# Seven opening pairs of a joint MLP over six PSUM banks in place of two, with twelve small operations on GpSimd in place of VectorE and two more tiles for sums

## The chip, the core and the metric

The kernel runs on one core of a Trainium2 chip. The metric is device time in microseconds for one launch; lower is better. The engines are named as the profile names them: PE is TensorE's matmul (PEld its weight load), DVE is VectorE, ACT is ScalarE, POOL is GpSimd, SP is SyncE, which here only issues DMAs.

## What is computed

One layer of a bidirectional encoder on 2048 tokens of 1024 features, in float32: a mixer of attention and convolution, a cross attention, a squared-ReLU MLP, and a final RMSNorm. The change lies in the MLP:

```python
u = rmsnorm(h, norm_mlp_g[l]) @ w_up[l]            # (2048, 1024) @ (1024, 4096)
h = h + jnp.square(jax.nn.relu(u)) @ w_down[l]     # (2048, 4096) @ (4096, 1024)
return rmsnorm(h, norm_final_g)
```

## The kernel before

The 2048 tokens are handled as four passes of 512 tokens. Everything is kept transposed: a tile has 128 features on its partitions and 512 tokens along its free axis. Passes 0 and 1 have an MLP each. Passes 2 and 3 share one, the joint MLP, which multiplies a 2 x 2 block matrix of weights by a 2 x 2 block matrix of activations with seven block products in place of eight (the Strassen-Winograd scheme).

**Operands.** Each product is done in three matmuls of half-width numbers: every operand is split into a high part (float16) and a low part (the rest, float16), and high x high, high x low and low x high are summed in PSUM. `prod` (lines 1788 to 1792) does one block product: four k steps of 128 features by three matmuls, 12 matmuls of 128 x 512, all into one PSUM bank.

**The seven blocks of activations** are b11, b21 (pass 2, its first and last 512 features), b22 (pass 3, its last 512 features) and four sums t1, t2, t3, t4. Each has four k tiles, and each k tile a high tile `Y..h` and a low tile `Y..l`. b11 and b21 are made while pass 2 is finished. The other five are made in the loop over k at lines 1768 to 1786, once pass 3's norm is known. For each k this loop makes two normalized tiles `n[0]`, `n[1]` (line 1772), then t1 = n0 - yn2 (1775), t2 = n1 - t1 (1776), t3 = n1 - n0 (1781), t4 = yn2' - t2 (1784), all on VectorE, and splits b22, t2, t1, t3 and t4 with `split_to` (lines 1723 to 1725): ScalarE copies the tile to float16 (1724), VectorE subtracts this from the tile and writes the low part (1725). The tiles for n and the sums come from `yt_` (line 1760), six buffers under one tag; each k needs six.

**Opening pairs.** The 4096 columns of `w_up` are handled as 16 pairs: a column block i of 128 with block i + 16. The loop at lines 1894 to 1898 runs ahead of the main loop for the first PRO = 7 pairs, with the part that needs only b11 and b21, so that it can run before the five other blocks exist. For each pair:

- the weight tile is loaded and split into high and low parts (`wpair`, lines 1798 on ScalarE and 1799 on VectorE); the even pairs have two buffers in one pool and the odd pairs two in another;
- `first_product` (1822): `prod` of b11 into a bank of kind `b1`, then ScalarE copies the bank to the tile `c1` (1826), which a GpSimd DMA writes to memory;
- `second_product` (1829): `prod` of b21 on top, in the same bank; then `squared` (1811): ScalarE takes the Relu from the bank (1812), which is the bank's last reader, and squares it (1813) into the tile `r11`, which a GpSimd DMA writes to memory.

The tiles c1 and r11 share six buffers (`wt_`). The kind `b1` has the banks 0 and 1, used in turn.

**Main loop.** `up_pair` (1836) runs for all 16 pairs. It loads two weight tiles, forms sums of them on VectorE (1844 to 1848), splits three sets (uu for t4; us for t2 and t1; ut for t3 and b22) and runs the products t4, then of the pair before the last product (`rest`, b22), then t2, t1, t3, with banks 2 and 3 (`b2`), 4 and 5 (`b3`), 6 and 7 (`b4`). For the first seven pairs it reads c1 and r11 back; for the others it runs the first and second product itself.

**Order.** The program text doesn't set the order of work. The kernel is traced, and a planner orders each engine's instructions by their place in the text and by a timeline that it simulates; each engine then runs its own list in that order and waits on semaphores where an operand or a buffer isn't there yet. An instruction that waits holds up all that stand behind it on its engine. A change in the buffers or in the engine of an operation can so give another order from there on.

**Memory.** The pool of the blocks and the pool `pm` of the working tiles stand where the pools of the closed stage `dense` stood.

Of the kernel before, what the change touches and what calls it, by code (L numbers as in the profile page):

```python
# [10 lines left out]
F32 = mybir.dt.float32  # L11
# [5 lines left out]
ALU = mybir.AluOpType  # L17
# [4 lines left out]
P = 128  # L22
# [25 lines left out]
def hybrid_layer(ctx, tc, A, out):  # L48
    nc = tc.nc
    ACT, DVE, POOL, PE = nc.scalar, nc.vector, nc.gpsimd, nc.tensor  # L50

    def pool(name, space=None, stack=ctx, side="left"):
        kw = {"reuse_waits": "tile", "side": side} if space is None else {"space": space}
        return stack.enter_context(tc.tile_pool(name=name, bufs=1, **kw))

    def dma(o, i, q=None):
        return (q or nc.sync).dma_start(o, i)  # L57
# [7 lines left out]
    banks = {"mm": (0, 1, 2, 5), "a": (3, 4), "sq": (6,), "c": (7,)}  # L65
# [199 lines left out]
    def wcols(w, c0, n=P, rows=None):  # L265
        v = w.rearrange("(k p) m -> p k m", p=P)
        return v[:, :, c0:c0 + n] if rows is None else v[:, rows[0]:rows[1], c0:c0 + n]
# [1446 lines left out]
    Y = {}  # L1714

    def half_room(pl, shape, **kw):
        t = pl.tile([shape[0], 2 * shape[1]] + list(shape[2:]), F16, **kw)
        return t[:, 0:shape[1]]
# [4 lines left out]
    def split_to(b, k, src):  # L1723
        ACT.copy(Y[b]["h"][k], src)
        DVE.tensor_tensor(Y[b]["l"][k], src, Y[b]["h"][k], op=ALU.subtract)
# [29 lines left out]
    pm = pool("up_work", stack=y_st)  # L1755

    def wt_(name, dtype=F32):
        return pm.tile([P, 512], dtype, tag="w", name=name, bufs=6)

    def yt_(name):  # L1760
        return pm.tile([P, 512], F32, tag="y", name=name, bufs=6)

    def late_tile(b, k):
        t = Y.setdefault(b, {"h": [], "l": []})
        for q in "hl":
            t[q].append(half_room(ybl[0], [P, 512], tag=f"{b}{q}{k}", name=f"Y{b}{q}{k}"))

    for k in range(4):
        n = [yt_(f"yn3_{k}{i}") for i in range(2)]
        for i in range(2):  # L1770
            kk = 4 * i + k
            DVE.scalar_tensor_tensor(n[i], h3[kk], gml[:, kk:kk + 1], rsbs[3], op0=ALU.mult, op1=ALU.mult)
        split_to("b22", k, n[1])
        t1b, t2b = yt_(f"yt1_{k}"), yt_(f"yt2_{k}")
        DVE.tensor_tensor(t1b, n[0], yn2[k], op=ALU.subtract)
        DVE.tensor_tensor(t2b, n[1], t1b, op=ALU.subtract)
        split_to("t2", k, t2b)
        late_tile("t1", k)
        split_to("t1", k, t1b)
        t3b = yt_(f"yt3_{k}")  # L1780
        DVE.tensor_tensor(t3b, n[1], n[0], op=ALU.subtract)
        split_to("t3", k, t3b)
        t4b = yt_(f"yt4_{k}")
        DVE.tensor_tensor(t4b, yn2[4 + k], t2b, op=ALU.subtract)
        late_tile("t4", k)
        split_to("t4", k, t4b)

    def prod(o, w, b, first):
        for k in range(4):
            for x, (i, q) in enumerate(((0, "h"), (0, "l"), (1, "h"))):  # L1790
                PE.matmul(o, w[i][:, k, :], Y[b][q][k], start=first and k + x == 0, stop=k == 3 and x == 2,
                          skip_group_check=not first)

    def halves(t):
        return [tuple(x[:, 4 * i:4 * i + 4, :] for x in t) for i in range(2)]
# [5 lines left out]
    def wpair(pl, t, name, shape=(P, 8, P)):  # L1801
        hi, lo = (half_room(pl, shape, tag=f"w{q}", name=f"w{q}_{name}", bufs=2) for q in ("hi", "lo"))
        scaled(hi, lo, t, mc[:, 0:1])
        return hi, lo

    def wraw(src, name):
        raw = wp.tile([P, 8, P], F32, tag="raw", name=f"raw_{name}", bufs=2)
        dma(raw, src)
        return raw

    def squared(r, src, j):
        ACT.activation(r, src, AF.Relu, scale=mc[:, 6:7])
        ACT.activation(r, r, AF.Square, accum_out=racc[:, j:j + 1])

    def keep_r(b, i, t):
        dma(rscr[b, i], t, nc.gpsimd)
# [5 lines left out]
    def first_product(i, a11):  # L1822
        b1 = ps("b1", f"b1_{i}")
        prod(b1, a11, "b11", True)
        c1 = wt_(f"c1_{i}")
        ACT.copy(c1, b1)
        return b1, c1

    def second_product(i, b1, a12):
        prod(b1, a12, "b21", False)  # L1830
        r11 = wt_(f"r11_{i}")
        squared(r11, b1, 4 * i)
        keep_r("b11", i, r11)
        return r11
# [56 lines left out]
        return rest  # L1891

    early_pairs = [True] * PRO
    for i in range(PRO):
        a1, a2 = halves(wpair(wq if i % 2 else wp, wraw(wcols(w_up, i * P), f"ua{i}"), f"ua{i}"))
        b1, c1 = first_product(i, a1)
        dma(cscr1[i], c1, nc.gpsimd)
        second_product(i, b1, a2)
    prev = lambda: None
    for i in range(NP):  # L1900
        prev = up_pair(i, early_pairs[i] if i < PRO else None, prev)
# [204 lines left out]
```

## Time and profile before

| | us |
|---|---|
| median of 3 runs | 2777.54 |
| lowest and highest of the runs | 2776.03, 2783.64 |
| the profiled execution, its time | 2774.07 |
| its span in the profile | 2772.3 |

The profiled execution is one execution on its own, and the views give positions in microseconds from the start of its span. A row of the order of time has the start, the duration, the engine, the line of the kernel, the operation, the tile written and the tiles read (buffer numbers left out), and in square brackets how long the engine had stood idle before it and what ended that. A row of groups has busy time and the mean duration of one behind the first bar, and idle time ahead of them behind the second. Matmuls overlap: one lasts 0.38 us, and the next starts 0.22 us after it. The opening pairs' first matmul starts at 2136.87; the main loop's last ends at about 2442.

### The profile page before, as it was taken

How to read it: one execution, taken by the hardware profiler on the slowest of the kernel's cores; microseconds unless marked ns; L12 is line 12 of the kernel's file. 1: busy time of each engine (PE TensorE's matmuls, PEld its weight loads, DVE VectorE, ACT ScalarE, POOL GpSimd, SP SyncE). 2: the span in 40 equal slices, each digit the busy share in tenths (PEclk: the TensorE clock that was granted, in tenths of full speed). 3: DMA queues.
4: the chain of work that ended last, by engine and by line, in shares of the span. 5: the costliest groups of instructions: out<-in, count | busy, mean ns of one | idle time of the engine just before them, and what ended most of it. 6: DMA issues, size and time to landing. Idle time of an engine off the chain costs nothing.

```text
span 2772.3 us, 40744 instructions
## 1 busy us (share of the span) xinstructions
PE 2661.1 (96%) x14787; PEld 1831.0 (66%) x14787; DVE 1918.8 (69%) x3508; ACT 1359.5 (49%) x2354; POOL 589.4 (21%) x807
## 2 busy tenths in 40 slices
PE   7899999988999999999999999999999999989998
PEld 4444457876777878788777777877887444434444
DVE  4568726665788876578976477756475887767776
ACT  6742217655454333434455555564343545545445
POOL 6474313543102212200111201121010122200000
PEclk9999999999999999999999999999999999999999
DMA  7874457887636666766457766764633564485553
GB/s 252 217 200 113 135 182 200 244 238 229 200 114 204 203 220 208 246 215 208 133 177 225 240 210 201 238 226 158 190 114 126 178 205 167 168 304 170 171 189 110
DMA packets 459816, 535.68 MB, mean 193 GB/s; under 512 B 98172, under 2 KB 329200, under 8 KB 459616
## 3 DMA queue, kind: packets, MB, share of 16 engines
q1 hardware_dynamic: 420992, 406.52, 48.5%
q0 software_dynamic: 36752, 123.06, 12.7%
q10 hardware_dynamic: 1872, 3.52, 0.3%
q8 instruction: 116, 1.90, 0.3%
q14 instruction: 84, 0.69, 0.1%
HBM read 384.46 MB, written 148.52 MB: 192 GB/s over the span
## 4 chain that ended last, share of the span: by engine, by line
PE 60%; DMA 13%; issue 11%; ACT 5%; DVE 5%; POOL 4%; SPq 2%; POOLq 0%; ACTq 0%; DVEq 0%
PE dn L270 4%; PE dn L271 4%; PE dn L272 4%; PE up L270 3%; PE up L272 3%; PE up L271 3%; PE lin L270 2%; PE lin L272 2%; PE lin L271 2%; SPq L57 2%; PE x L270 2%; PE x L271 2%; PE x L272 2%; PE xs L270 2%; PE xs L272 2%
## 5 line engine op out<-in xcount | busy, mean ns | idle before, releaser
L287 DVE SCALAR_TENSOR_TENSOR cacc<-cu,cwu,cacc 128x512 f32<-128x512 f32 x480 | 395.6, 826 | 6.8
L1032 ACT ACTIVATE sm<-sm,o 128x256 f32<-128x256 f32 (+1 forms) x384 | 159.2, 466 | 115.3 <-DVE o L1031 114.8
L270 PE MATMUL dn<-hhh,whi_d 128*128 128x512 f32 x512 | 202.1, 405 | 5.8 <-ACT hhh L1591 3.5
L270 PE MATMUL up<-mh,whi_u 128*128 128x512 f32 x512 | 203.9, 399 | 1.7 <-ACT whi_u L1567 1.7
L271 PE MATMUL dn<-hhl,whi_d 128*128 128x512 f32 x512 | 200.6, 394 | 0.8 <-DVE hhl L1592 0.8
L272 PE MATMUL up<-mh,wlo_u 128*128 128x512 f32 x512 | 200.0, 391 | 0.0
L272 PE MATMUL dn<-hhh,wlo_d 128*128 128x512 f32 x512 | 199.9, 393 | 0.0
L271 PE MATMUL up<-ml,whi_u 128*128 128x512 f32 x512 | 199.6, 390 | 0.0
L1042 DVE TENSOR_TENSOR pl<-pt,ph 128x512 f16<-128x512 f32 x160 | 109.6, 685 | 80.3 <-ACT ph L1041 79.8
L1031 DVE CUSTOM_DVE_ANT_0 sm<-s,mask 128x256 f32<-128x256 f32 (+1 forms) x384 | 126.6, 373 | 33.5 <-DMA oscr<-o 11.8
L1041 ACT CAST ph<-pt 128x512 f16<-128x512 f32 x160 | 92.2, 576 | 77.0 <-PE pt L1038 76.3
L1606 DVE TENSOR_TENSOR h<-h,dn 128x512 f32<-128x512 f32 x128 | 85.9, 682 | 55.6 <-PE dn L272 55.0
L247 POOL TENSOR_TENSOR nr<-st_v,mhalf 128x4 f32<-128x4 f32 x12 | 13.2, 1098 | 513.2 <-DVE st_v L243 513.2
L270 PEld LDWEIGHTS dn<-hhh,whi_d 128*128 128x128 f32 x512 | 95.5, 188 | 25.8 <-ACT hhh L1591 5.2
L272 PEld LDWEIGHTS dn<-hhh,wlo_d 128*128 128x128 f32 x512 | 96.6, 189 | 20.3
L270 PEld LDWEIGHTS up<-mh,whi_u 128*128 128x128 f32 x512 | 96.2, 188 | 20.6 <-ACT whi_u L1567 2.0
L271 PEld LDWEIGHTS dn<-hhl,whi_d 128*128 128x128 f32 x512 | 96.7, 189 | 19.6 <-DVE hhl L1592 1.8
L272 PEld LDWEIGHTS up<-mh,wlo_u 128*128 128x128 f32 x512 | 96.1, 188 | 20.5
L271 PEld LDWEIGHTS up<-ml,whi_u 128*128 128x128 f32 x512 | 96.3, 188 | 18.6
L270 PE MATMUL o<-cath,whi_o 128*128 128x512 f32 x256 | 103.0, 403 | 4.3 <-ACT whi_o L261 3.6
L272 PE MATMUL o<-cath,wlo_o 128*128 128x512 f32 x256 | 101.5, 398 | 1.4 <-DVE wlo_o L262 1.4
L1038 PE MATMUL pt<-ident,sm 128*128 128x128 f32 x640 | 100.1, 274 | 2.7 <-ACT sm L1032 2.5
(647 smaller groups left out, 7835.8 us busy)
## 6 DMA issues: line engine op xcount, KB each, us to landing
raw_u<-in_w_up_dram SPq DMA_DIRECT2D x64, 512.0 KB
raw_d<-in_w_down_dram SPq DMA_DIRECT2D x64, 512.0 KB
k<-kscr SPq DMA_DIRECT2D x32, 640.0 KB
raw_a<-ascr SPq DMA_DIRECT2D x32, 512.0 KB
raw_b<-bscr SPq DMA_DIRECT2D x32, 512.0 KB
lou<-wlo_u POOLq DMA_DIRECT2D x32, 512.0 KB, 5.4
lod<-wlo_d POOLq DMA_DIRECT2D x32, 512.0 KB, 5.5
wlo_u<-lou SPq DMA_DIRECT2D x32, 512.0 KB
```

Source lines behind the costliest of these rows:

```text
L57: return (q or nc.sync).dma_start(o, i)
L247: last["pow"] = POOL.tensor_tensor(dst, v, mhalf.to_broadcast([P, v.shape[1]]), op=ALU.pow)
L270: PE.matmul(o, lh, rh, start=first, stop=False)
L271: PE.matmul(o, lh, rl, start=False, stop=False)
L272: last["pe"] = PE.matmul(o, ll, rh, start=False, stop=end)
L287: DVE.scalar_tensor_tensor(acc, u[:, t:t + 512], cwu[:, c, t:t + 1], acc, op0=ALU.mult, op1=ALU.add)
L1031: last["dve"] = DVE.tensor_tensor_reduce(dst, so, mask[:, 256 * m:256 * m + nk], 1.0, 3e38, ALU.add, ALU.min, mn)
L1032: last["act"] = ACT.activation(dst, dst, AF.Exp, bias=mn, scale=-1.0)
L1038: last["pe"] = PE.transpose(pt[:, j, :], sm[:, j, :], ident)
L1041: ACT.copy(ph, pt)
L1042: DVE.tensor_tensor(pl, pt, ph, op=ALU.subtract)
L1606: last["dve"] = DVE.tensor_tensor(hs[m], hs[m], pt, op=ALU.add)
```

## The change

Four things change: VectorE's subtraction that makes a low part is done by GpSimd for the blocks b22 and t3, four tiles each (`split_by_pool`); the difference t3 = n1 - n0 is done by GpSimd, four times; the buffers of `yt_` become eight; and the opening pairs use six banks for `b1`, 0 to 5 in turn, after which `b1` has 0 and 1 again. The copies to float16 stay on ScalarE. Pair 6 is then the first to use a bank for the second time.

```diff
+    YB = 8
+
     def yt_(name):
-        return pm.tile([P, 512], F32, tag="y", name=name, bufs=6)
+        return pm.tile([P, 512], F32, tag="y", name=name, bufs=YB)
...
+    def split_by_pool(b, k, src):
+        ACT.copy(Y[b]["h"][k], src)
+        POOL.tensor_tensor(Y[b]["l"][k], src, Y[b]["h"][k], op=ALU.subtract)
+
     for k in range(4):
...
-        split_to("b22", k, n[1])
+        split_by_pool("b22", k, n[1])
...
-        DVE.tensor_tensor(t3b, n[1], n[0], op=ALU.subtract)
-        split_to("t3", k, t3b)
+        POOL.tensor_tensor(t3b, n[1], n[0], op=ALU.subtract)
+        split_by_pool("t3", k, t3b)
...
     early_pairs = [True] * PRO
+    banks.update(b1=(0, 1, 2, 3, 4, 5))
     for i in range(PRO):
...
         second_product(i, b1, a2)
+    banks.update(b1=(0, 1))
     prev = lambda: None
```

## The prediction

> **What bounds the kernel now.** I read the page first, then the stretch of the seven opening pairs and what follows, in windows (columns: from and to, length, then the busy time of PE, PEld, DVE, ACT and POOL, which is GpSimd, the granted TensorE clock, DMA share, GB/s).
>
> ```profile
> span 2772.3 us, 40744 instructions
> ...
> PE 2661.1 (96%) x14787; PEld 1831.0 (66%) x14787; DVE 1918.8 (69%) x3508; ACT 1359.5 (49%) x2354; POOL 589.4 (21%) x807
> ```
>
> ```profile
> 2142.06:2178.94 36.88, 31.10 (x148) 14.25 (x146) 32.63 (x52) 24.92 (x46) 6.50 (x11) 1.00 0.39 125
> 2178.94:2187.79 8.85, 8.85 (x43) 4.00 (x41) 6.89 (x11) 4.49 (x8) 1.08 (x2) 1.00 0.55 187
> 2187.79:2212.40 24.61, 24.61 (x114) 11.04 (x113) 16.59 (x23) 9.42 (x17) 3.76 (x7) 1.00 0.73 236
> ```
>
> TensorE is busy 96% of the span, so time is won only where it stands still. In the opening pairs it does: 36.88 - 31.10 = 5.78 us. In the 33 us behind them it has no gap at all, so whatever is late there delays everything after it.
>
> The order of time on PE shows the cause:
>
> ```profile
> 2147.26 0.38 PE L1791 MATMUL b<-Yb11h,whi_ua 128*128 128x512 f16 x1 [1.21 <-ACT r L1812]
> ...
> 2149.85 0.38 PE L1791 MATMUL b<-Yb21h,whi_ua 128*128 128x512 f16 x1
> ...
> 2152.22 0.38 PE L1791 MATMUL b<-Yb21h,wlo_ua 128*128 128x512 f16 x1
> 2154.20 0.38 PE L1791 MATMUL b<-Yb11h,whi_ua 128*128 128x512 f16 x1 [1.60 <-ACT r L1812]
> ...
> 2161.14 0.38 PE L1791 MATMUL b<-Yb11h,whi_ua 128*128 128x512 f16 x1 [1.60 <-ACT r L1812]
> ...
> 2173.19 0.39 PE L1791 MATMUL b<-Yt4h,whi_uu 128*128 128x512 f16 x1 [0.60 <-ACT whi_uu L1798]
> ```
>
> A product is 12 matmuls: from 2149.85 to 2152.22 there are 11 steps, 0.2155 each, so a product takes 2.59 us. Each stall stands ahead of a first product (Yb11) and is ended by the Relu of line 1812, which reads the bank that this product needs: with two banks, pair i+2 waits until pair i has left. What keeps the Relu late is the order on ScalarE:
>
> ```profile
> 2145.49 1.15 ACT L1798 ACTIVATE whi_ua<-raw_ua,wscl 128x1024 f16<-128x1024 f32 x1 [5.24 <-PE b L1791]
> 2146.54 0.67 ACT L1812 ACTIVATE r<-b,wscl 128x512 f32<-128x512 f32 x1
> 2147.11 0.57 ACT L1826 COPY c<-b 128x512 f32<-128x512 f32 x1
> ```
>
> A weight cast comes first, waiting for the buffer that the same second product frees.
>
> **Six banks.** They remove the Relu from the path: 5.78 us of idle, and since a waiting PE also drains (0.38 for the last matmul against 0.2155 in the flow, 0.16 at each of five restarts), 6.6 us in all. The weights don't take its place: four pairs have their own buffers, and the casts of pairs 4, 5 and 6 follow the second products of pairs 0, 1 and 2, which come at least two products (5.2 us) before use; cast 1.15 and low part 1.28 fit. The third to sixth banks are those that the main loop's pair 0 and 1 use for t2 and t1, but those products come after t4, by when the Relus of pairs 2 to 5 are done. By itself this edit is worth 0 to -6.6, if what PE does next is ready 6.6 us sooner.
>
> **Is it ready?** That is VectorE's work, the sums and low parts of the seven blocks. Its window (DVE is the fourth figure, 35.71) and groups (count, busy us, mean ns of one):
>
> ```profile
> 2148.20:2184.20 36.00, 31.43 (x144) 13.76 (x143) 35.71 (x55) 25.53 (x47) 6.33 (x12) 1.00 0.49 160
> ```
>
> ```profile
> L1725 DVE TENSOR_TENSOR Yb22l<-yn,Yb22h 128x512 f16<-128x512 f32 x4 | 2.7, 683 | 0.0
> ...
> L1781 DVE TENSOR_TENSOR yt<-yn,yn 128x512 f32<-128x512 f32 x4 | 2.7, 683 | 0.0
> ...
> L1725 DVE TENSOR_TENSOR Yt3l<-yt,Yt3h 128x512 f16<-128x512 f32 x4 | 2.7, 682 | 0.0
> ```
>
> VectorE is busy 35.71 of 36.00 us, and the end of this stream is used at once:
>
> ```profile
> 2182.89 0.69 DVE L1844 TENSOR_TENSOR s<-raw_ub 128x512 f32<-128x512 f32 x1 [0.25 <-DMA raw_ub<-in_w_up_dram]
> 2183.50 0.68 DVE L1725 TENSOR_TENSOR Yt4l<-yt,Yt4h 128x512 f16<-128x512 f32 x1
> 2184.10 0.68 DVE L1847 TENSOR_TENSOR s<-raw_um,raw_ub 128x512 f32<-128x512 f32 x1
> ...
> 2188.53 0.75 DVE L1799 SCALAR_TENSOR_TENSOR wlo_uu<-raw_ub,wscl,whi_uu 128x512 f16<-128x512 f32 x1 [2.42 <-ACT whi_uu L1798]
> ```
>
> ```profile
> 2187.77 0.72 ACT L1798 ACTIVATE whi_uu<-raw_ub,wscl 128x512 f16<-128x512 f32 x1 [1.14 <-PE b L1791]
> ```
>
> ```profile
> 2189.73 0.38 PE L1791 MATMUL b<-Yt4h,whi_uu 128*128 128x512 f16 x1
> ```
>
> The last low part of t4 ends at 2184.18; pair 1's low weights end at 2189.28 and PE starts pair 1 at 2189.73. So PE reaches pair 1 with 0.45 us to spare, and until then it fills in with the last second product. A PE that is 6.6 us early only waits for VectorE. This is why the second edit decides.
>
> **Twelve operations to GpSimd** (b22's and t3's low parts, t3's difference, four each). VectorE is rid of 12 x 0.60 (the step from 2183.50 to 2184.10) = 7.2 us. What GpSimd takes, from its groups:
>
> ```profile
> L1168 POOL TENSOR_TENSOR ld<-ld,ce 128x512 f32<-128x512 f32 x30 | 39.3, 1330 | 0.0
> ...
> L420 POOL TENSOR_TENSOR xl<-xv,xh 128x512 f16<-128x512 f32 x32 | 37.5, 1186 | 26.5 <-ACT xh L419 26.4
> ...
> L57 POOL DMA_DIRECT2D c1s<-c x7 | 4.0, 566 | 108.6 <-ACT c L1826 108.6
> ```
>
> 8 x 1.19 (the same form as L420's) + 4 x 1.33 = 14.8 us, and with the 14 DMA issues of the opening pairs (0.57 each) 22.8 of 36 us. GpSimd has room, and b22 and t3 are used last of a pair's blocks, so being slow costs nothing there. The DMAs queued behind these operations (c1 and r11 to memory) have readers only in the main loop; the tiles that they free come round after three pairs, over 15 us.
>
> But the two engines don't run independently. Just before, GpSimd made eight sums while VectorE worked:
>
> ```profile
> 2043.73 5.46 POOL L1744 TENSOR_TENSOR yn<-Yb11h,Yb11l 128x512 f32<-128x512 f16 x4 [35.34 <-PE o L272]
> 2049.15 6.42 POOL L1744 TENSOR_TENSOR yn<-Yb21h,Yb21l 128x512 f32<-128x512 f16 x4
> ```
>
> ```profile
> 2039.75 0.69 DVE L1436 TENSOR_TENSOR ssumo<-ssumo,sq 128x512 f32<-128x512 f32 x1
> ...
> 2046.51 1.66 DVE L1436 TENSOR_TENSOR ssumo<-ssumo,sq 128x512 f32<-128x512 f32 x1
> 2048.08 0.68 DVE L1466 TENSOR_TENSOR h<-o,res 128x512 f32<-128x512 f32 x1
> ...
> 2051.77 1.65 DVE L1436 TENSOR_TENSOR ssumo<-ssumo,sq 128x512 f32<-128x512 f32 x1
> ```
>
> The same sum takes 0.69 before GpSimd starts and 1.66 and 1.65 beside it, 0.97 more; line 1466, which reads one operand from PSUM, keeps 0.68. All the operations of VectorE's stream here read two operands from SBUF, as line 1436 does. I take 0.97 of VectorE's time for each GpSimd operation, by that nearest row. Bounds: below, nothing lost if GpSimd finds only gaps; above, its whole 1.33. So the twelve give VectorE -7.2 to +8.8, and by the value taken 12 x 0.97 - 7.2 = +4.4 us.
>
> [...]
>
> **Two more y tiles** cost nothing: VectorE's stream has only 0.29 us of gaps that a tile could have caused, and the pool grows by 4 KB to 60 KB a partition, in the room of a closed stage that had 76 KB. They cover for the operands that GpSimd now holds longer; without them VectorE would wait for a tile as soon as GpSimd is one k behind.
>
> **The sum.** Pair 1's low weights, 2189.28 before: minus the gaps 0.25 and 2.42 (the second waited for a weight buffer held by pair 6's second product, which now ends long before), minus 7.2, plus 11.6 = 2191.0. That is 1.7 us later than before, although PE passed the opening pairs 6.6 us sooner. From there PE has no gap, so the delay stays: 2774.07 (the profiled execution: 2772.3 of span and 1.8 around it) + 1.7 = 2775.8. The median of the runs is 3.5 above that execution, so the forecast is 2777.5 + 1.7 = 2779.2. Its own range, with 0.56 to 1.2 a piece in place of 0.97 (0.56: on average over the eight sums, of which some fell into gaps or beside line 1466), is -3.2 to +4.5: 2774 to 2782.
>
> **Rivals.** (1) The gain comes through. If GpSimd costs VectorE at most 0.3 a piece, the stream ends at 2183 and PE never waits: -6.6, 2770.9. If PE's lead also removes the next stalls, such as
>
> ```profile
> 2213.51 0.38 PE L1791 MATMUL b<-Yb22h,whi_ut 128*128 128x512 f16 x1 [1.01 <-DVE r L1870]
> ```
>
> it is -7.6, and less than 2769 with two more like it. For it speaks that GpSimd may fall into waits of VectorE for ScalarE that a lighter stream would have; against it, 35.71 of 36.00.
>
> (2) Slower. The order on each engine is written by a planner that counts every engine by itself, so PE's order places late blocks where VectorE would have them unhindered. PE runs dry at about 2181 (the opening pairs are over at 2174.9, which is 2178.94 less 6.6 and plus one second product still open there; then 27 matmuls of t4, t2, t1 for three of the four k, 5.8 us) and waits in one piece for the fourth k. Behind long waits the clock drops:
>
> ```profile
> 2445.28 0.32 PE L255 MATMUL rtop<-ident,cw 128*128 128x128 f32 x1 [3.15 <-DVE cw L1904]
> 2449.08 1.87 PE L270 MATMUL p<-bh_p,whi_p 128*128 128x512 f16 x4 [3.48 <-ACT bh_p L1798]
> ```
>
> ```profile
> 2450.00:2455.00 5.00, 5.00 (x16) 1.83 (x15) 4.81 (x7) 2.44 (x4) 0.00 (x0) 0.60 1.02 333
> ```
>
> After waits of 3.15 and 3.48 with one transpose between them the granted clock is 0.60 over the next 5 us, a loss of 2.0; after 1.60 it stayed 1.00. With the full 1.33 a piece the stream is 16.0 - 7.2 - 2.7 = 6.1 late, and with the clock's 2.0 this is 8.1; one late matmul that stands ahead of a ready second product (2.59) makes it 10.7: 2788. It decides from 1.1 a piece on, together with a wait over some 3 us. For it: VectorE's stream leaves GpSimd no gaps. Against: before, PE was ordered around late blocks well.
>
> [...]
>
> (3) It doesn't do what it says: the planner's order keeps first and second products alternating behind the same ScalarE casts, and the banks stay unused. Then only VectorE's +4.4 counts: 2782.
>
> **How the numbers follow.** 0.3% is 8.3 us, about what a measurement of this kernel can tell from no change: under 2769.2 is faster, over 2785.9 slower. Forecast 0.36 (0.03 of it slower), rival 1 0.25 (0.17 faster), rival 2 0.31 (0.29 slower), rival 3 0.08 (0.03 slower). Together faster 0.17, same 0.48, slower 0.35. The range 2768 to 2791 reaches to rival 1's end and past rival 2, leaving out a tenth on either side at most.
>
> **What would show it.** Right: no bracket "ACT r L1812" on PE ahead of Yb11 products; VectorE operations of 1.5 to 1.7 us between 2148 and 2190 where 0.68 stood; a PE wait ended by a DVE or by POOL in that stretch; pair 1's first t4 product near 2191. Wrong in the gain's favour: VectorE's operations stay at 0.68 beside GpSimd's, and pair 1 starts near 2183. Wrong towards slower: a PE wait over 3 us there, with a granted clock under 1.00 behind it. Differences far from this stretch would mean that the planner's order changed elsewhere, which none of the terms holds.

## The result, and the profile after

| | us |
|---|---|
| before, median of 22 runs | 2776.41 |
| after, median of 22 runs | 2786.31 |
| ratio, with 95% interval | 1.0031 [1.0021, 1.0040] |
| after, the profiled execution, its time | 2784.71 |
| its span in the profile | 2782.8 |

The changed kernel is slower by 0.31%, about 8.6 us (9.9 between the medians); the prediction had 1.7 us (2779.2), with a range up to 2791. Lines from 1768 on stand six or more further down in the changed kernel: the difference t1 is L1781 (before 1775), the products are L1797 (1791), the weights' casts and low parts L1804 and L1805 (1798, 1799), the Relu L1818 (1812), the copy of c L1832 (1826), the sum r22, which reads the bank that b22's product needs, L1876 (1870). GpSimd's low parts are L1772, its difference L1787.

The page of the changed kernel, its first lines:

```profile
span 2782.8 us, 40737 instructions
...
PE 2667.4 (96%) x14787; PEld 1834.3 (66%) x14787; DVE 1925.0 (69%) x3496; ACT 1359.0 (49%) x2354; POOL 608.9 (22%) x819
```

VectorE has twelve instructions fewer and is busy 6.2 us longer (1918.8 before), so what was left of its work costs more. Where the time went is read from windows, from the first matmul of the opening pairs on: 100 us, and from there to the main loop's last matmul (columns as in the prediction: stretch, length, then PE, PEld, DVE, ACT, POOL, clock). Before:

```profile
2136.87:2236.87 100.00, 93.21 (x434) 42.34 (x434) 78.11 (x115) 54.49 (x96) 17.42 (x31) 1.00 0.56 185
2236.87:2441.97 205.10, 200.34 (x925) 90.20 (x923) 147.14 (x202) 110.76 (x195) 45.04 (x84) 1.00 0.51 175
```

and after:

```profile
2138.03:2238.03 100.00, 86.83 (x386) 38.04 (x386) 76.33 (x95) 50.27 (x89) 34.90 (x40) 0.97 0.50 166
2238.03:2452.17 214.14, 210.64 (x973) 94.92 (x970) 152.90 (x209) 115.01 (x203) 46.83 (x87) 1.00 0.52 177
```

In its first 100 us PE does 48 matmuls fewer, at 0.2155 each 10.3 us of work. 6.4 of these are idle time (93.21 - 86.83); most of the rest is the clock (0.97). The second part does the missing work and gains 1.3 of it back in stalls that it no longer has (idle 4.8 before, 3.5 after). So the **stretch** from first to last matmul goes from 305.1 to 314.1; it starts 1.2 us later and what follows takes 0.3 more. The stretch is the measure below, since its start moves by some us from one execution to the next for reasons that lie ahead of it.

The order of time of the changed kernel, PE's waits among the opening pairs and behind them, with what ended two of them on ScalarE, VectorE and GpSimd:

```profile
2162.40 0.39 PE L1797 MATMUL b<-Yb11h,wlo_ua 128*128 128x512 f16 x1 [1.78 <-DVE wlo_ua L1805]
2162.27 1.75 DVE L1781 TENSOR_TENSOR yt<-yn,yn 128x512 f32<-128x512 f32 x1
2164.05 0.62 ACT L1724 CAST Yt1h<-yt 128x512 f16<-128x512 f32 x1 [2.25 <-DVE yt L1781]
2164.57 1.14 ACT L1804 ACTIVATE whi_ua<-raw_ua,wscl 128x1024 f16<-128x1024 f32 x1
2165.77 0.39 PE L1797 MATMUL b<-Yb11h,whi_ua 128*128 128x512 f16 x1 [1.04 <-ACT whi_ua L1804]
2171.47 0.39 PE L1797 MATMUL b<-Yb11h,wlo_ua 128*128 128x512 f16 x1 [1.90 <-DVE wlo_ua L1805]
...
2172.39 1.71 POOL L1787 TENSOR_TENSOR yt<-yn,yn 128x512 f32<-128x512 f32 x1
2172.90 1.75 DVE L1781 TENSOR_TENSOR yt<-yn,yn 128x512 f32<-128x512 f32 x1
2174.68 0.62 ACT L1724 CAST Yt1h<-yt 128x512 f16<-128x512 f32 x1 [2.13 <-DVE yt L1781]
...
2177.72 0.72 ACT L1804 ACTIVATE whi_uu<-raw_ub,wscl 128x512 f16<-128x512 f32 x1
2178.50 0.39 PE L1797 MATMUL b<-Yt4h,whi_uu 128*128 128x512 f16 x1 [2.11 <-ACT whi_uu L1804]
...
2179.92 0.63 PE L1797 MATMUL b<-Yb21l,whi_ua 128*128 128x512 f16 x1
...
2182.05 0.63 PE L1797 MATMUL b<-Yb21h,whi_ua 128*128 128x512 f16 x1
...
2193.82 0.69 DVE L1850 TENSOR_TENSOR s<-raw_ub 128x512 f32<-128x512 f32 x1 [2.85 <-DMA raw_ub<-in_w_up_dram]
2196.97 0.38 PE L1797 MATMUL b<-Yt4l,whi_uu 128*128 128x512 f16 x1 [1.41 <-DVE Yt4l L1725]
...
2223.28 0.38 PE L1797 MATMUL b<-Yb22h,whi_ut 128*128 128x512 f16 x1 [1.99 <-DVE r L1876]
```

This is to be read from the bottom of each chain up. Line 1781's difference t1, 0.68 before, takes 1.75 beside GpSimd's difference at 2172.39. ScalarE's copy of t1 stands at the head of ScalarE's list and waits 2.13 for it; three more copies and the weight cast `whi_uu` stand behind it in order; PE waits 2.11 for the cast. The same at 2162.27 to 2165.77 for pair 6's weights. Then the clock: from 2179.92 to 2182.05 there are five steps of 0.43 instead of 0.2155, and the granted clock from 2179.54 to 2182.97 is 0.52. The first 100 us hold 16 matmuls of 0.5 to 0.7 us, eight behind this wait (and one of 0.44 two matmuls later) and eight behind the last one shown, at 0.21 more each 3.4 us. Idle 6.4 and clock 3.4 make 9.8 of the 10.3. No product waits for a Relu (L1818) any more.

Over the whole stream twelve operations of VectorE are held up, as many as GpSimd has. Each takes 0.89 to 1.07 us more than its kind takes elsewhere, 11.7 us together, 0.97 on average.

Where VectorE's stream begins has moved too. PE's sums and transposes for the norm, before:

```profile
2142.06 0.95 PE L1445 MATMUL nps<-ones,ssumx 128*128 128x1 f32 x8
2145.45 0.60 PE L255 MATMUL nrb<-ident,nr 128*128 128x128 f32 x4
```

and after:

```profile
2145.17 0.95 PE L1445 MATMUL nps<-ones,ssumx 128*128 128x1 f32 x8
2151.80 0.60 PE L255 MATMUL nrb<-ident,nr 128*128 128x128 f32 x4
```

The transposes `nrb` come 8.6 us after the first matmul before and 13.8 after: with six banks the planner has products ready to put ahead of them. The blocks start 3.7 us later (15.0 against 11.3 us after the first matmul).

### The profile page after: what moved, and what is told of

The parts are those of the page before. It is cut to its first block, busy times and chain, and to the rows that moved or that the text cites. A ratio compares the mean times of both kernels' runs of the same rounds, so it can differ in the third digit from the quotient of the medians.

```text
span 2782.8 us, 40737 instructions
## 1 busy us (share of the span) xinstructions
PE 2667.4 (96%) x14787; PEld 1834.3 (66%) x14787; DVE 1925.0 (69%) x3496; ACT 1359.0 (49%) x2354; POOL 608.9 (22%) x819
## 4 chain that ended last, share of the span: by engine, by line
PE 63%; DMA 15%; DVE 7%; issue 6%; ACT 5%; SPq 2%; POOL 2%; ACTq 0%; DVEq 0%; POOLq 0%
PE b L1797 5%; PE dn L270 3%; PE dn L271 3%; PE dn L272 3%; PE up L270 3%; PE up L272 3%; PE up L271 3%; SPq L57 2%; DMA raw_d<-in_w_down_dram 2%; PE x L270 2%; PE x L271 2%; PE x L272 2%; PE lin L270 2%; PE lin L272 2%; PE lin L271 2%
## 5 line engine op out<-in xcount | busy, mean ns | idle before, releaser
L247 POOL TENSOR_TENSOR nr<-st_v,mhalf 128x4 f32<-128x4 f32 x12 | 13.2, 1098 | 518.6 <-DVE st_v L243 518.6
L1144 POOL TENSOR_TENSOR ce<-csm,o 128x8 f32<-128x8 f32 x15 | 7.6, 509 | 443.7 <-DVE csm L1143 443.7
```

The costliest lines, as they stand in the source:

```text
L247: last["pow"] = POOL.tensor_tensor(dst, v, mhalf.to_broadcast([P, v.shape[1]]), op=ALU.pow)
```

## The experiments

Twelve kernels, each with a profile and 6 to 12 timed runs. Their runs of the kernel before had medians of 2775.86 (for the first four), 2774.95 (the next four), 2774.34 (banks with zero fills, b22 only, norm with GpSimd) and 2773.69 (difference only). In the table the stretch is from the order of time, "stream end" is when VectorE's last low part of t4 starts, counted from the first matmul, idle is 100 us less PE's busy time in the first 100, and slow matmuls are those of 0.5 to 0.7 us there. The stretch is that of one execution of each kernel, and a single group of eight slow matmuls makes 1.7 us of it.

| kernel | ratio, 95% interval | stretch | stream end | idle | slow matmuls |
|---|---|---|---|---|---|
| before | | 305.1 | 46.6 | 6.8 | 0 |
| after | 1.0031 [1.0021, 1.0040] | 314.1 | 58.2 | 13.2 | 16 |
| six banks | 0.9995 [0.9984, 1.0006] | 303.1 | 52.4 | 5.0 | 0 |
| eight tiles | 0.9999 [0.9987, 1.0012] | 304.4 | 46.5 | 6.8 | 0 |
| six banks, eight tiles | 1.0012 [0.9999, 1.0024] | 304.6 | 52.5 | 5.1 | 0 |
| GpSimd, eight tiles, two banks | 1.0059 [1.0043, 1.0075] | 321.1 | 50.8 | 16.1 | 30 |
| six banks, norm before pair 2 | 0.9999 [0.9986, 1.0012] | 304.2 | 47.6 | 5.3 | 8 |
| six banks, norm before pair 1 | 0.9982 [0.9969, 0.9995] | 301.7 | 45.2 | 4.5 | 8 |
| two banks, zero fills | 1.0001 [0.9987, 1.0016] | 305.4 | 37.1 | 7.6 | 0 |
| two banks, eight low parts | 1.0024 [1.0010, 1.0037] | 310.7 | 47.3 | 10.1 | 16 |
| six banks, zero fills | 0.9995 [0.9985, 1.0006] | 302.1 | 44.0 | 5.3 | 8 |
| six banks, b22's low parts only | 1.0013 [1.0000, 1.0026] | 305.0 | 53.3 | 6.8 | 0 |
| six banks, t3's differences only | 1.0005 [0.9988, 1.0021] | 306.0 | 54.3 | 6.9 | 0 |
| after, with norm before pair 1 | 1.0037 [1.0024, 1.0050] | 315.5 | 46.7 | 11.7 | 22 |

### The parts alone

The change taken apart in four kernels: the banks alone

```diff
+    banks.update(b1=(0, 1, 2, 3, 4, 5))
     for i in range(PRO):
...
+    banks.update(b1=(0, 1))
```

> Six banks alone; VectorE keeps all twelve operations, six y tiles. Theory A (two costs: VectorE held up by GpSimd, and the norm of pass 3 pushed behind pair 2's first product on PE, so that the normalized tiles start about 3.7 us later): the stalls ended by the Relu of line 1812 are gone, the normalized tiles start about 3.7 us later than before, VectorE's operations stay at 0.68, the 2.7 us gap in VectorE's stream closes, pair 1's first t4 product comes about 1 us later; total +1 us (between -2 and +4). Rival B (the order that six banks give costs everything): +8 to +9 us. Rival C (GpSimd costs everything, the banks help): -3 to -6 us.

the twelve operations on GpSimd with the eight tiles, and two banks as before

```diff
-        split_to("b22", k, n[1])
+        split_by_pool("b22", k, n[1])
...
-        DVE.tensor_tensor(t3b, n[1], n[0], op=ALU.subtract)
-        split_to("t3", k, t3b)
+        POOL.tensor_tensor(t3b, n[1], n[0], op=ALU.subtract)
+        split_by_pool("t3", k, t3b)
```

> The twelve operations on GpSimd and eight y tiles, two banks as before. Theory A: the norm keeps its place, the Relu stalls stay, twelve VectorE operations take 0.9 to 1.0 us more each, VectorE's stream ends about 4.4 us later and pair 1's first t4 product 2 to 4.4 us later; total +2 to +5 us. Rival B: within 1 us of before. Rival C: +8 to +9 us.

the tiles alone

```diff
-        return pm.tile([P, 512], F32, tag="y", name=name, bufs=6)
+        return pm.tile([P, 512], F32, tag="y", name=name, bufs=8)
```

> Eight y tiles alone. Every theory: within 1.5 us of before, as VectorE's stream has hardly a gap that a tile could cause.

and banks and tiles together, without GpSimd.

> Six banks and eight y tiles, all twelve operations on VectorE. Theory A and rival B: as with six banks alone, within 1.5 us. Rival C: -3 to -6 us. Should the tiles matter only when PE runs ahead, this run would be faster than six banks alone by more than 2 us.

Banks and tiles, alone or together, leave the stretch within 2.0 us of before, below what the totals tell apart (some 3.5 us). The whole loss comes with GpSimd: +16.7 us of stretch with two banks (321.1 against 304.4), +9.5 with six (314.1 against 304.6). So beside GpSimd's operations the banks do save 7.0 us, though alone they save 2. None of the three theories had the size for GpSimd with two banks: the largest said +8 to +9 us. The order of time of the kernel with GpSimd and two banks:

```profile
2156.62 0.58 PE L1797 MATMUL b<-Yb11h,whi_ua 128*128 128x512 f16 x1 [4.75 <-ACT r L1818]
...
2159.57 2.28 DVE L1805 SCALAR_TENSOR_TENSOR wlo_ua<-raw_ua,wscl,whi_ua 128x1024 f16<-128x1024 f32 x1
2161.78 0.68 DVE L1782 TENSOR_TENSOR yt<-yn,yt 128x512 f32<-128x512 f32 x1
2162.49 0.62 ACT L1724 CAST Yt2h<-yt 128x512 f16<-128x512 f32 x1 [3.28 <-DVE yt L1782]
...
2165.78 0.68 ACT L1818 ACTIVATE r<-b,wscl 128x512 f32<-128x512 f32 x1
2166.51 0.58 PE L1797 MATMUL b<-Yb11h,whi_ua 128*128 128x512 f16 x1 [3.07 <-ACT r L1818]
...
2175.46 5.71 POOL L1772 TENSOR_TENSOR Yb22l<-yn,Yb22h 128x512 f16<-128x512 f32 x1 [3.21 <-ACT Yb22h L1771]
...
2177.23 0.59 PE L1797 MATMUL b<-Yb11h,whi_ua 128*128 128x512 f16 x1 [3.73 <-ACT r L1818]
2182.43 0.62 ACT L1771 CAST Yt3h<-yt 128x512 f16<-128x512 f32 x1 [4.16 <-POOL yt L1787]
...
2187.03 0.61 PE L1797 MATMUL b<-Yt2h,wlo_us 128*128 128x512 f16 x1 [1.32 <-DVE wlo_us L1805]
```

The Relu stalls of 1.6 us grow to 3.07 to 4.75, because the Relu stands on ScalarE behind a copy that waits for VectorE, held up in its turn, or for GpSimd itself. GpSimd is held up as well: a low part, 1.19 in the row of L420, took 5.71, and its difference then came late for ScalarE (4.16). Slow matmuls follow each of the three long PE waits, and eight more the wait of 1.32 for low weights; they are 30 in all (6.3 us), and with 9.3 more idle this is 15.6 of the 16.7. VectorE's own stream ends only 4.3 us later than in the kernel with tiles alone.

### Is it the norm, pushed back behind the products?

Six banks let products go ahead of the norm. Two kernels with six banks and nothing on GpSimd keep the first products of pairs 2 to 6, or of pairs 1 to 6, behind the norm's transposes on PE:

```diff
-        bcast_rows(rb, r, 4)
+        last["nrb"] = bcast_rows(rb, r, 4)
...
-        prod(b1, a11, "b11", True)
+        with ExitStack() as st:
+            if 2 <= i < PRO:
+                after(st, "nrb")
+            prod(b1, a11, "b11", True)
```

> Six banks, everything else as before; pair 2's first product and those after it are issued on PE behind the transposes that spread pass 3's norm, as they stood with two banks. Theory A (with six banks the norm is pushed behind pair 2's first product, and the late start of VectorE's stream eats what the banks give): the normalized tiles start 11.3 us behind the opening pairs' first matmul as before, in place of 15.0 with six banks alone; the stretch from that matmul to the main loop's last is 3 us shorter than with six banks alone (303.1), near 300; total -4 to -6 us against before. Rival (the weights of pairs 4 to 6 set the pace, the norm's place doesn't matter): as six banks alone, 302 to 304, total -1 to -3 us.

and with `1 <= i` in its place:

> As the run before, with pair 1's first product behind the norm's transposes too, so that the norm is asked for one product (2.6 us) earlier. Theory A: the normalized tiles start about 9 us behind the first matmul, the stretch is 1 to 2.5 us shorter again, near 298, PE waiting about 0.5 us for the sum of squares; total -5 to -8 us against before. Rival: no better than the run before.

The blocks start 11.3 and 9.1 us after the first matmul, as meant. From pair 2 on it gains nothing over the banks alone (304.2 against 303.1), though there a wait of 2.38 at b22's product and eight slow matmuls (1.7) lie in the way. From pair 1 on it makes 301.7, and 0.9982 of before, the only interval wholly under 1; it overlaps that of the banks alone, and neither stretch comes down to the 300 and 298 that were expected. Why not more is in the order of time of the second kernel:

```profile
2148.19 0.60 PE L255 MATMUL nrb<-ident,nr 128*128 128x128 f32 x4
...
2211.06 0.69 DVE L1847 TENSOR_TENSOR s<-raw_ub 128x512 f32<-128x512 f32 x1 [1.34 <-DMA raw_ub<-in_w_up_dram]
...
2214.74 0.69 DVE L1873 TENSOR_TENSOR r<-b,r 128x512 f32<-128x512 f32 x1
2215.48 0.38 PE L1791 MATMUL b<-Yb22h,whi_ut 128*128 128x512 f16 x1 [2.54 <-DVE r L1873]
...
2216.34 0.62 PE L1791 MATMUL b<-Yb22l,whi_ut 128*128 128x512 f16 x1
...
2219.31 0.60 PE L1791 MATMUL b<-Yb22h,wlo_ut 128*128 128x512 f16 x1
```

PE is through with the work ahead of this product of b22 4.2 us sooner than before, counted from the first matmul. There it waits for a sum of VectorE (L1873) that stands behind a sum of weights still on their way by DMA. The wait of 2.54 and the eight slow matmuls behind it (1.7) cost 4.2 us, where the kernel before lost 1.01.

### Is it the reads of SBUF?

The kernel with GpSimd and two banks once more, but GpSimd fills with zeros and reads nothing; it leaves out the low parts of b22 and t3 and the difference t3:

```diff
-        POOL.tensor_tensor(Y[b]["l"][k], src, Y[b]["h"][k], op=ALU.subtract)
+        POOL.memset(Y[b]["l"][k], 0.0)
...
-        POOL.tensor_tensor(t3b, n[1], n[0], op=ALU.subtract)
+        POOL.memset(t3b, 0.0)
```

> Two banks, eight y tiles, and the twelve GpSimd operations at their places, but as fills with zeros that read nothing: the low parts of b22 and t3 and the difference t3 are left out. Theory A (VectorE is held up because both engines read two operands from SBUF): no VectorE operation in the stretch over 0.8 us but the long ones at 1.28; the 16 us that the twelve subtractions cost are gone, total -1 to -6 us against before. Rival D (it is GpSimd's place in the chain, with its queue and the ScalarE copies that wait for it, that costs, whatever its operations read): +5 to +16 us.

and with the differences on VectorE again, eight low parts on GpSimd:

```diff
-        POOL.tensor_tensor(t3b, n[1], n[0], op=ALU.subtract)
+        DVE.tensor_tensor(t3b, n[1], n[0], op=ALU.subtract)
```

> Two banks, eight y tiles, the difference t3 back on VectorE, the eight low parts on GpSimd. Theory A in its simple form (each GpSimd operation costs alike): two thirds of 16 us, +9 to +12 us. Rival E (the ScalarE copy of t3 that waits for GpSimd's difference, and all that stands behind this copy, makes most of it): +2 to +5 us.

With zero fills none of VectorE's operations on the blocks is held up (0.68 to 0.69 for sums and low parts) and the loss is gone (305.4). But a fill waits for no operand and takes only 0.52 to 0.55. The eight fills of low parts run from 2138.82 to 2142.61, over 7 us ahead of the blocks, and not at their places; only the four fills of t3 run beside VectorE's stream. These four hold up none of its operations (the sums and low parts beside them take 0.68, two scalings in a row 1.40), where a difference that reads holds one up (1.75 for 0.68 in the changed kernel). So their place alone isn't the cause; the fills differ from the differences in that they read nothing, and in length (0.52 to 0.54 against 1.58 to 2.16 in the changed kernel). For the low parts the run takes away the reads, the length and the place together. Nothing is gained either, although VectorE's stream ends 9.5 us earlier than before (37.1 against 46.6). The order of time of that kernel:

```profile
2156.26 0.38 PE L1797 MATMUL b<-Yb11h,whi_ua 128*128 128x512 f16 x1 [1.93 <-ACT r L1818]
2163.72 0.38 PE L1797 MATMUL b<-Yb11h,whi_ua 128*128 128x512 f16 x1 [2.12 <-ACT r L1818]
...
2175.73 0.69 DVE L1725 TENSOR_TENSOR Yt4l<-yt,Yt4h 128x512 f16<-128x512 f32 x1
```

The Relu stalls stay, and with two banks they set the pace, not VectorE. The eight low parts cost 6.3 us of stretch against tiles alone (310.7 against 304.4), which lies between what the two theories said, and the four differences added to them the other 10 of the 16.7. With the eight low parts neither ScalarE nor PE waits for GpSimd. Eight operations of VectorE are held up, by 7.5 us together, and ScalarE's copies wait up to 2.95 us for VectorE, with the Relus behind them: there the loss came by VectorE.

The same zero fills in the changed kernel, where PE can run ahead:

> The changed kernel (six banks, eight tiles) with GpSimd's twelve operations as zero fills that read nothing: it leaves out the low parts of b22 and t3 and the difference t3. Theory (with six banks VectorE's stream is what decides, and only reads of SBUF hold it up): no VectorE operation of the blocks over 0.8 us, no PE wait on the opening weights over 1.2 us, and as VectorE is rid of 7.2 us, the stretch from the opening pairs' first matmul to the main loop's last is shorter than with banks and tiles alone (304.6): 300 to 303, time 0.9980 to 0.9993 of before. Rival (behind the opening pairs b22's sums r22 decide, which stand behind other VectorE work and a DMA): 304 to 305.5, time within 0.1% of before. If the cost is in what GpSimd's instructions do to the order or to the matmuls' operands and not in their reads, the stretch stays near the changed kernel's 314.

Here the lighter stream, which ends 8.5 us earlier than with banks and tiles alone, does pay: 302.1 against 304.6 in these two executions, while the intervals of the two ratios overlap. It pays 2.5 and no more for the reason seen above, in the order of time of this kernel:

```profile
2169.15 0.55 POOL L1787 MEMSET yt<- 128x512 f32 x1
2169.16 0.69 DVE L1781 TENSOR_TENSOR yt<-yn,yn 128x512 f32<-128x512 f32 x1
...
2200.47 0.38 PE L1797 MATMUL b<-Yb22h,whi_ut 128*128 128x512 f16 x1 [1.04 <-DVE r L1876]
2216.27 0.38 PE L1797 MATMUL b<-Yb22h,whi_ut 128*128 128x512 f16 x1 [2.69 <-DVE r L1876]
```

A sum that takes 1.75 beside GpSimd's difference takes 0.69 beside its fill. In the main loop b22's products lose 3.7 us again, and eight slow matmuls follow the second wait.

### How the price grows

Four of the twelve operations, with six banks and eight tiles: b22's low parts alone

```diff
-        POOL.tensor_tensor(t3b, n[1], n[0], op=ALU.subtract)
-        split_by_pool("t3", k, t3b)
+        DVE.tensor_tensor(t3b, n[1], n[0], op=ALU.subtract)
+        split_to("t3", k, t3b)
```

> The changed kernel with only b22's four low parts on GpSimd; t3's difference and low parts are VectorE's again. Theory that the price goes by the number of operations (0.97 each, less the 0.6 taken off): a third of the changed kernel's loss against banks and tiles alone, 304.6 + 3.2 = 307.8, time 1.0022 of before, four VectorE operations of 1.6 us. Rival (the price is a threshold: only a PE wait of 2 us or more also costs clock, and four operations leave each wait under that): stretch 304 to 305.5, no half-rate matmuls beyond the three of banks and tiles alone, time within 0.1% of that kernel's.

and t3's differences alone

```diff
-        split_by_pool("b22", k, n[1])
+        split_to("b22", k, n[1])
...
-        split_by_pool("t3", k, t3b)
+        split_to("t3", k, t3b)
```

> The changed kernel with only t3's four differences on GpSimd; all low parts are VectorE's. As many operations as with b22's low parts alone (stretch 305.0), but ScalarE's copy of t3 reads their result, and weight casts stand behind that copy in ScalarE's order. Theory that the place counts: stretch 307 to 311, time 1.002 to 1.003 of before, waits of ScalarE for GpSimd's t3 of over 1 us and PE waits of 2 us or more. Rival that the number counts: stretch 304 to 305.5 and time 1.001, as for b22's low parts alone, so that the price comes only when the groups of four are together.

For VectorE the price goes by the number: four of its operations are held up beside b22's four low parts, four beside the differences and twelve beside all twelve, by 3.9, 3.9 and 11.7 us, about 0.97 each. The end of its stream isn't as clean a measure (0.8, 1.8 and 5.7 us later than with banks and tiles alone), since the order of its operations differs, and the changed kernel's holds the wait of 2.85 for a DMA shown at 2193.82. For PE the price doesn't go by the number: +0.4, +1.4 and +9.5 of stretch. In the order of time of the kernel with b22's low parts alone:

```profile
2163.83 0.39 PE L1797 MATMUL b<-Yb11h,wlo_ua 128*128 128x512 f16 x1 [0.52 <-DVE wlo_ua L1805]
...
2172.82 6.24 POOL L1772 TENSOR_TENSOR Yb22l<-yn,Yb22h 128x512 f16<-128x512 f32 x1
...
2179.66 0.39 PE L1797 MATMUL b<-Yt4h,wlo_uu 128*128 128x512 f16 x1 [0.71 <-DVE wlo_uu L1805]
```

the weights' waits are there, but small (0.52 and 0.71), with no slow matmuls behind them. GpSimd pays instead (6.24 for one low part), and nobody waits for b22's. Both rivals that spoke of a threshold or of the group held, the second not exactly: 306.0 lies half a us over its bound. (The three half-rate matmuls that the first expectation gives to banks and tiles alone are rows of 0.59 us that hold two matmuls each; that kernel has none.)

Last, the changed kernel with the norm ahead of pair 1, as in the kernel that was faster:

> The changed kernel with the first products of pairs 1 to 6 put behind the norm's broadcast on PE, so that the blocks start earlier (the order that by itself made six banks faster, stretch 301.7). Theory that GpSimd's price is paid in full wherever the norm stands (VectorE's operations held up, weights of the last opening pairs late): 301.7 + 9.5 = 311, time 1.002 to 1.003 of before, about eleven VectorE operations of 1.6 us. Rival that the changed kernel lost mostly because six banks let the norm start 3.7 us later, so that VectorE's stream met the weights of pairs 5 and 6: stretch 303 to 306, time 0.999 to 1.000, and no PE wait of 2 us or more within the opening pairs.

The price is paid in full and more, 13.8 us against the same kernel without GpSimd (301.7): that the norm came later wasn't what cost the changed kernel its time. VectorE's stream ends at 46.7, only 1.5 after that kernel's, so the end of the stream doesn't show the loss at all. The order of time does:

```profile
2163.43 0.61 PE L1797 MATMUL b<-Yb11h,whi_ua 128*128 128x512 f16 x1 [3.69 <-ACT whi_ua L1804]
2165.30 4.73 POOL L1772 TENSOR_TENSOR Yt3l<-yt,Yt3h 128x512 f16<-128x512 f32 x1
2170.06 5.79 DVE L1778 SCALAR_TENSOR_TENSOR yn<-h,wscl,rsb 128x512 f32<-128x512 f32 x2 [1.05 <-POOL Yt3l L1772]
2176.37 2.28 DVE L1805 SCALAR_TENSOR_TENSOR wlo_ua<-raw_ua,wscl,whi_ua 128x1024 f16<-128x1024 f32 x1
2178.71 0.39 PE L1797 MATMUL b<-Yb11h,wlo_ua 128*128 128x512 f16 x1 [3.87 <-DVE wlo_ua L1805]
```

GpSimd's low part of t3 takes 4.73 in place of 1.19 beside six operations of VectorE without a gap between them, then VectorE waits itself 1.05 for it, since it holds the tile for the next block. The next low weights stand behind that and behind two scalings (the row of x2 reaches from the start of the first to the end of the second, 1.4 where nothing is in the way). The two last 5.79, and in that time GpSimd does three operations of 1.16 to 1.28. PE loses 3.87. Here even eight tiles were too few.

## Why the prediction was right and where it failed

**Six banks remove the Relu stalls: right.** No product of the changed kernel waits for L1818. Alone the banks gave 2.0 us of stretch, within the 0 to -6.6 given. But the 5.78 us weren't all Relu: the stall of 0.60 at 2173.19, which the prediction shows, is a wait for the weight cast `whi_uu`. The same wait is the 2.11 of the changed kernel.

**VectorE's price: right in kind and in size.** The prediction took 0.97 for each GpSimd operation and so +4.4 for VectorE; twelve operations are held up, by 11.7 us together, which less 7.2 is +4.5. Beside the zero fills that ran within VectorE's stream, which read nothing, none is held up (t1's differences take 0.68 and 0.69 there).

**The sum at pair 1's low weights: this step failed.** It gave 1.7 us later than before. Counted from the first matmul they end at 60.2 us (2198.18) in place of 52.4, 7.7 later. The sum had nothing for the blocks' start, which came 3.7 later. It also took away two gaps: the one of 2.42 did go, but the one of 0.25, a wait for a DMA, became 2.85. And by its own 0.45 us that PE had to spare, 1.7 on VectorE would have been 1.3 on PE.

**"The weights don't take its place": this step failed.** It counted time from second product to use (5.2 us) against the cast and the low part by themselves (1.15 and 1.28), and left out what both stand behind: on ScalarE the copies of sums, on VectorE the held-up stream. The waits of 1.78, 1.04 and 1.90 in the changed kernel are for weights of pairs 5 and 6, the 2.11 is for the main loop's first.

**"A PE that is early only waits for VectorE", at the stream's end: failed with it.** The +4.4 was charged once, at pair 1's low weights. The delay doesn't wait for the end: operations held up in the middle hold up copies on ScalarE (2.13 and 2.25 in the changed kernel, 3.28 with two banks), and behind these a weight cast or a Relu. The kernel with GpSimd and norm first loses 13.8 us with its stream end only 1.5 later. And VectorE's 35.71 of 36.00 wasn't what bound the kernel before: with a stream 9.5 us shorter it took as long (two banks, zero fills).

**The clock: only in rival 2.** The forecast had none of the 3.4 us. Rival 2, the slower one, came nearest in time (2788 against 2786.31), but this is partly luck. By its own condition, 1.1 for an operation, it shouldn't have come, as 0.97 was measured; and there was no long wait for t4's fourth block at 2181, but pieces of 1.0 to 2.1 at the weights, and drops behind pieces of 2.11 and 1.99. The step that put the drop over some 3 us was off.

**The range held, the forecast didn't.** The measured 2786.31 lies 7.1 us over the forecast of 2779.2 and within 2768 to 2791 only because the range reaches past rival 2. It lies just over the 2785.9 that the prediction set for a slower kernel, to which it gave 0.35.

**Not foreseen:** the norm put behind pair 2's first product (3.7 us for the blocks). It isn't what made the changed kernel slow, since that kernel with the norm kept before pair 1 is no faster. What the norm's place costs by itself stays open: with it kept before pair 2 the stretch was no shorter than with the banks alone, but that execution holds a group of slow matmuls.

**"From there PE has no gap, so the delay stays":** nearly; 1.3 of 10.3 us came back. What was late next was b22's product, after VectorE's sum L1876: 1.99 in the changed kernel, 2.54 and 2.69 where PE came earlier. Which part of the four differences' 10 us with two banks is ScalarE's wait for GpSimd and which is VectorE's delay wasn't separated.

## What to carry to other kernels

An engine that is busy 99% of a stretch isn't thereby what bounds it (VectorE was, 35.71 of 36.00 us, and with its stream ending 9.5 us sooner the stretch was 305.4 against 305.1); take its work away (zero fills in place of the operations) before you pay to lighten it. When an operation is moved to an engine beside which the old one was seen to slow down (here by 0.97 us for each operation moved), price the delay at each consumer in the middle of the stream, above all where urgent work stands behind a copy in an engine's order (here a weight cast behind the copy of t1, 2.11 us of PE), and not once at its end. Watch for the size of single waits on TensorE as well as for their sum: here waits of 0.52 and 0.71 us at the weights left the stretch as it was (305.0 against 304.6), while one of 1.99 us had eight slow matmuls behind it, 1.7 us more (one of 2.12 had none).

## What the runs showed of the hardware

Slow matmuls follow waits shorter than the prediction took from the trace of before, but not each time. In the stretches of these kernels a group of them stood behind single waits of 1.99, 2.11, 2.24, 2.31, 2.38, 2.54 and 2.69 us, and behind all of 3.07 to 4.75 but one, the 3.11 in the main loop of the kernel with GpSimd and two banks. There were none behind 2.12, 2.63 and two of 2.17. Below 1.99 only one wait had a group behind it, the 1.32 shown for GpSimd with two banks, where one of 0.70 ended 2.4 us earlier. So the length of a wait alone doesn't decide it; what else does, no run shows. The slow matmuls begin within 1.1 us of the restart, and most groups last about 3.4 us (2216.34 to 2219.74 in the kernel with the norm before pair 1), at 0.43 a matmul. Over the changed kernel's two groups the granted clock is 0.52 (2179.54 to 2182.97) and 0.51 (2223.71 to 2227.10).

GpSimd and VectorE hold each other up, not one the other: beside a subtraction of GpSimd VectorE loses about 1 us (1.75 for 0.68), while GpSimd's low parts, 1.19 in the row of L420, took 4.73, 5.71 and 6.24 beside VectorE's stream. Where GpSimd had three operations one after the other, VectorE lost more (5.79 for two scalings of 1.40 together). That rests on rows of the changed kernel, and of those with GpSimd and two banks, with b22's low parts alone, and with the norm before pair 1 and GpSimd.
